# A two-block network on one core, its engines' orders taken from the scheduler's other timing model

## The chip, the cores and the metric

One core of a Trainium2 chip runs the kernel. It has a matrix engine (PE, with weight loads shown apart as PEld), a vector engine (DVE), a scalar engine (ACT), a general engine (POOL) and a sync engine (SP) that only issues transfers. The metric is the device time of one execution in microseconds (us), the median of several runs.

## The reference

Input `x` is 256 tokens of width 1024, all in fp32. The first block is two hybrid layers, the second one mixer layer with routed experts.

```python
def first_block(x, ...):
    for l in range(2):                       # hybrid_layer
        z = rms_norm(x, norm_g) @ w_in       # 2840 columns
        y_a = rg_lru(conv(rg_x)) * silu(rg_gate)
        y_b = nsa(q, k_c, v_c, k_s, v_s, k_w, v_w, ...) * silu(nsa_gate)
        x = x + concat([y_a, y_b]) @ w_out
    return x

def second_block(x, ...):
    p = rms_norm_2(x, norm_mix_w) @ w_in     # 3336 columns
    x = x + concat([rwkv7_mixer(...), fox_mixer(...)]) @ w_out
    h = rms_norm_2(x, norm_ffn_w)
    return x + hierarchical_moe(h, ...)      # top 2 of 64 experts
...
    hid = silu(xblk @ w_gate[e]) * (xblk @ w_up[e])   # 1024 x 512 each
    return hid @ w_down[e]
```

Each of the 64 experts has three matrices of 2 MB, so the experts' weights are some 400 MB.

## The kernel before

The source is one program for the framework's tracer. `model` (L1819) calls the stages in order: `hybrid` twice, `mixer`, then `moe`. Tiles live in one large on-chip array, `arena`, whose places are handed out in Python while the source is traced, in seven blocks `b0` to `b6` of 4096 words, and in PSUM buffers by tag (`mm`, `tp`, `sc`, `ot`, two buffers each).

Dense weights of the first three layers come in blocks through a ring of five of those seven blocks. POOL issues the load of a block (`issue`, L256). Its high part is rounded as it lands. Then `weights_steps` makes the low part: ACT writes the negated high part (L286) and POOL issues a second load of the same words that adds to it (L291). The products of high and low parts are three matmul passes (`mm3_steps`, L304). So each weight block passes through POOL, the DMA engines, ACT, POOL and the DMA engines again before PE can use it all.

Dense products of one branch are used as side work for the other. `step(cols)` runs the generator `self.side` until it has put in matmuls of so many columns; the amounts are constants of the file (`HA` to `HD`, `FA` to `FG`). In `hybrid` the main line is the attention (q, k and v with L501, L502, L507 and L508 as the evictions, L526 and L527 as those of the compressed keys and gates, `rope` L407 to L410, transposes L540, `softmax` L801 to L814, `turned` L822), the side line is `rg_part`. In `mixer` the main line is a triangular solve of 32x32 matmuls (L1057), the side line the remaining projections; L860 to L863 prepare its parameters, which `mixer_params` has SP load (L833).

The experts run in 16 groups of four. Ten slots of 2 MB hold their weights: block 6 and three stretches of the arena as they come free in the mixer, the other six blocks at its end. `fill` has SP issue the next load (L1542, L1557, L1550) as soon as a slot is free in the source; on the chip SP waits in front of each for the last reader of that slot. `experts` gathers rows (L1579), multiplies by gate and up (L1608), and by down (L1639), and adds the result back (L1647, L1649).

What sets the order. Tracing gives one list of instructions with their dependences. When the `tile.TileContext` closes, its scheduler plays this list through a timing model: whenever an engine is free in the model, it takes among the instructions whose inputs the model holds ready the one that comes first in the source. What an engine took one after another becomes its instruction stream, and the waits on other engines are written into it. On the chip an engine goes through its stream in that order, and an instruction that waits holds back those behind it. An instruction marked `keep_in_program_order` is held behind what was traced before it on its engine: the scalings of q and k (L534), the first matmul of the mixer's pinned steps and of each round of the solve, the first gather and one weight block per layer (`PB`).

## Time and profile before

| | us |
|---|---|
| median of 3 runs | 1512.48 (1506.65 to 1514.28) |
| profiled execution | 1520.82 |
| its span, first to last instruction | 1519.1 |
| PE busy | 1217.5 (80%) |
| DVE busy | 423.2 (28%) |
| ACT busy | 316.2 (21%) |
| POOL busy | 148.0 (10%) |
| bytes moved by DMA | 510.27 MB, mean 336 GB/s |

The profile is of one execution. Busy time of PE counts pipelined matmuls as they overlap and isn't PE at its peak. The profile's 40 slices are 38 us each. The first 16 of them are the three dense layers and the routing, the rest are the experts. In the lines of a timeline, the bracket at the end is the idle time of the engine ahead of that instruction, and what ended it.

### The profile page before, as it was taken

To read this page: it belongs to the slowest core of one execution; us is meant where nothing else is said; L and a number is where in the kernel's file an instruction comes from. 1 tells how busy PE (TensorE), PEld (TensorE's weight loads), DVE (VectorE), ACT (ScalarE), POOL (GpSimd) and SP (SyncE) were. 2 spreads that over 40 slices of the span, in tenths; PEclk is the share of its full clock that TensorE was granted. 3 is DMA by queue.
4 is the path that set the end of the run, shared out by engine and by line. 5 is a ranking of instruction groups with operands and counts; after the bars stand their busy time and mean duration, and the time that the engine had idled before them with its cause. 6 is when DMAs were issued, how large, how long until landed. Compare 5 with 4: busy or idle time off the path is not lost.

```text
span 1519.1 us, 20669 instructions
## 1 busy us (share of the span) xinstructions
PE 1217.5 (80%) x8695; PEld 678.3 (45%) x8695; DVE 423.2 (28%) x1250; ACT 316.2 (21%) x748; POOL 148.0 (10%) x201
## 2 busy tenths in 40 slices
PE   6799889889778998976876876877868768768774
PEld 5777677676656685431331331322313313313311
DVE  6546346533525465210110101101101101101010
ACT  4448346736223412000000000000000000000000
POOL 5221322122302300000000000000000000000000
PEclk9979989988899898987987888978878979878897
DMA  8976999749746668999999999999999999999996
GB/s 322 229 190 153 254 281 246 196 129 253 177 99 149 158 230 331 428 427 428 428 428 428 428 428 427 427 428 428 427 428 427 427 429 428 427 429 428 423 408 229
DMA packets 62005, 510.27 MB, mean 336 GB/s; under 512 B 5948, under 2 KB 6076, under 8 KB 34388
## 3 DMA queue, kind: packets, MB, share of 16 engines
q1 hardware_dynamic: 42180, 418.26, 65.7%
q0 software_dynamic: 19728, 90.65, 24.7%
q8 instruction: 70, 1.15, 0.3%
q14 instruction: 27, 0.22, 0.0%
HBM read 507.83 MB, written 1.05 MB: 335 GB/s over the span
## 4 chain that ended last, share of the span: by engine, by line
PE 39%; DMA 33%; DVE 3%; issue 3%; POOL 1%; ACT 0%; POOLq 0%; ACTq 0%; DVEq 0%
DMA slot<-in_wu 19%; DMA arena<-in_wu 12%; PE sc L1608 10%; PE ot L1639 8%; PE tp L1579 8%; PE mm L304 5%; DMA arena<-in_wd 1%; PE tp L1630 1%; DVE arena L1626 1%; PE ot L1057 1%; DMA w<-in_w_in 1%; PE mm L1647 0%; POOL w L291 0%; PE sc L1057 0%; PE sc L1374 0%
## 5 line engine op out<-in xcount | busy, mean ns | idle before, releaser
L1608 PE MATMUL sc<-slot,arena 128*32 128x512 f32 x1424 | 326.6, 741 | 132.5 <-DMA slot<-in_wu 81.4
L1608 PE MATMUL sc<-arena 128*32 128x512 f32 x624 | 187.2, 737 | 61.2 <-DMA arena<-in_wu 37.7
L1608 PEld LDWEIGHTS sc<-slot,arena 128*32 128x32 f32 x1424 | 70.0, 131 | 307.6 <-issue 122.5
L304 PE MATMUL mm<-hT,w 128*128 128x256 f32 (+1 forms) x936 | 142.3, 309 | 4.7 <-DMA w<-in_w_in 3.2
L304 PEld LDWEIGHTS mm<-hT,w 128*128 128x128 f32 (+1 forms) x936 | 127.8, 207 | 17.9 <-issue 9.2
L1579 PEld LDWEIGHTS tp<-arena 128*128 128x128 f32 x512 | 124.3, 334 | 17.9 <-issue 17.9
L1579 PE MATMUL tp<-arena 128*128 128x128 f32 x512 | 128.5, 406 | 2.4 <-DVE arena L1577 2.4
L1639 PE MATMUL ot<-slot,arena 128*32 128x512 f32 x704 | 124.4, 596 | 2.8 <-DMA slot<-in_wd 2.0
L286 ACT ACTIVATE w<-w 128x512 fp32r<-128x512 f32 (+1 forms) x181 | 99.0, 603 | 92.5 <-DMA w<-in_w_in 58.1
L1608 PEld LDWEIGHTS sc<-arena 128*32 128x32 f32 x624 | 40.7, 131 | 166.3 <-issue 76.3
L304 PE MATMUL mm<-w,hT 128*128 128x512 f32 (+1 forms) x432 | 105.1, 396 | 10.7 <-DVE arena L502 4.4
L304 PEld LDWEIGHTS mm<-w,hT 128*128 128x128 f32 x432 | 78.5, 200 | 27.8 <-issue 8.8
L1626 DVE SCALAR_TENSOR_TENSOR arena<-arena,sc 128x512 f32<-128x512 f32 x16 | 11.0, 688 | 265.8 <-PE sc L1608 265.8
L1625 DVE SCALAR_TENSOR_TENSOR arena<-arena,sc 128x512 f32<-128x512 f32 x16 | 11.0, 688 | 265.3 <-ACT arena L1624 265.3
L1649 DVE TENSOR_TENSOR arena<-arena,mm 128x512 f32<-128x512 f32 x64 | 44.0, 688 | 118.2 <-PE mm L1647 118.2
L304 PE MATMUL mm<-w,y 128*128 128x512 f32 x288 | 75.5, 408 | 0.9 <-DVE arena L747 0.9
L1639 PE MATMUL ot<-arena 128*32 128x512 f32 x320 | 71.9, 608 | 3.6 <-DMA arena<-in_wd 3.6
L291 POOL DMA_DIRECT2D w<-in_w_in x67 | 59.5, 946 | 136.5 <-ACT w L286 125.5
L1632 ACT COPY arena<-tp 128x512 f32<-128x512 f32 x16 | 9.4, 586 | 302.7 <-PE tp L1630 302.7
L1644 ACT COPY arena<-ot 128x512 f32<-128x512 f32 x32 | 18.8, 586 | 250.3 <-PE ot L1639 250.3
L1647 PE MATMUL mm<-arena 128*128 128x512 f32 x128 | 64.6, 628 | 1.6 <-ACT arena L1644 1.4
L1624 ACT ACTIVATE arena<-sc 128x512 f32<-128x512 f32 x16 | 9.6, 597 | 261.0 <-PE sc L1608 261.0
(386 smaller groups left out, 1246.8 us busy)
## 6 DMA issues: line engine op xcount, KB each, us to landing
slot<-in_wg SPq DMA_DIRECT2D x47, 2048.0 KB, 31.1
slot<-in_wu SPq DMA_DIRECT2D x42, 2048.0 KB, 33.5
slot<-in_wd SPq DMA_DIRECT2D x42, 2048.0 KB, 35.3
arena<-in_wu SPq DMA_DIRECT2D x22, 2048.0 KB, 33.4
arena<-in_wd SPq DMA_DIRECT2D x18, 2048.0 KB, 34.9
arena<-in_wg SPq DMA_DIRECT2D x17, 2048.0 KB, 32.0
w<-in_w_in POOLq DMA_DIRECT2D x29, 1024.0 KB, 8.7
w<-in_w_in POOLq DMA_DIRECT2D x58, 512.0 KB, 8.8
```

Of the source, the lines that this page charges most:

```text
L286: a = self.S.activation(lo[:, sl], hi[:, sl].bitcast(F32), AF.Copy, scale=-1.0)
L291: self.G.dma_start(lo[:, sl], src[:, sl], accum_op=OP.add)
L304: ins = self.T.matmul(out, lhsT=lhs[k][a], rhs=rhs[k][b], start=(first and i == 0 and k == 0), stop=(last and i == 2 and k == n - 1))
L1057: ins = T.matmul(o[qd(q, d), h * 32:(h + 1) * 32], lhsT=lhs[qd(q, d), h], rhs=rhs[qd(q, d), h], start=True, stop=True)
L1579: ins = T.matmul(self.rows[k // 4][:, k % 4 * 128:(k % 4 + 1) * 128], lhsT=hv[:, tt, k], rhs=D[:, tt], start=(tt == 0 and k % 4 == 0), sto ...
L1608: T.matmul(dst[32 * j:32 * j + 32], lhsT=XT[:, k, 32 * j:32 * j + 32], rhs=w(j), start=(k == 0), stop=(k == 7))
L1626: V.scalar_tensor_tensor(hid, hid, 0.5, pu, OP.mult, OP.mult)
L1630: T.transpose(ps[:, k * 128:(k + 1) * 128], hw[:, k], self.ident)
L1639: T.matmul(py[h][32 * j:32 * j + 32], lhsT=HT[:, k, 32 * j:32 * j + 32], rhs=w(j), start=(k == 0), stop=(k == 3))
L1644: S.copy(Y[:, cs], py[h])
L1647: T.matmul(pc, lhsT=DT[:, tt * 128:(tt + 1) * 128], rhs=Y[:, cs], start=True, stop=True)
L1649: V.tensor_tensor(xs, xs, pc, OP.add)
```

## The change

The one call that opens the scheduler's context gets an argument. With it the scheduler plays the list through the other, finer of its two timing models, when it works out each engine's order. The list itself, its dependences, the pinned instructions, the constants and the places in the arena stay as they were. What can come out otherwise is the order of PE, DVE, ACT, POOL and SP, which of the two PSUM buffers of a tag a tile gets, and the waits that follow from both.

```diff
@@ -1874,6 +1874,6 @@
     out = nc.dram_tensor("out", (1, 256, 1024), F32, kind="ExternalOutput").ap()
-    with tile.TileContext(nc) as tc:
+    with tile.TileContext(nc, schedule_with_timeline_sim=True) as tc:
         model(tc, A, out)
```

## Rows read from the trace of the kernel before

**Rows 1.** The page's 40 slices: busy tenths of the DMA engines

```profile
DMA  8976999749746668999999999999999999999996
```

**Rows 2.** By stretch: busy us of PE, PEld, DVE, ACT, POOL; clock; DMA share; GB/s

```profile
0.00:600.00 600.00, 521.01 (x4927) 412.42 (x4931) 306.01 (x1004) 272.92 (x669) 147.98 (x201) 0.91 0.78 212
600.00:1457.00 857.00, 663.69 (x3592) 258.74 (x3588) 113.05 (x241) 40.92 (x75) 0.00 (x0) 0.85 1.00 426
1457.00:1519.00 62.00, 32.77 (x188) 7.10 (x180) 4.13 (x6) 2.36 (x4) 0.00 (x0) 0.82 0.78 299
```

**Rows 3.** Chain of waits in order of time: start us, us, what

```profile
599.33 13.91 PE sc L1608 x128
...
682.44 30.72 DMA arena<-in_wu
...
740.82 31.11 DMA arena<-in_wu
```

**Rows 4.** Timeline of SP's queue near 590 us: start us, us, instruction

```profile
581.53 0.92 SPq L1557 DMA_DIRECT2D slot<-in_wd  x2
601.24 2.08 SPq L1557 DMA_DIRECT2D arena<-in_wd  x2
```

**Rows 5.** Timeline of PE, [idle before <-releaser]: gaps in the first stage

```profile
41.91 6.46 PE L304 MATMUL mm<-w,hT 128*128 128x280 f32 x48 [0.30 <-ACT arena L512]
...
58.20 1.12 PE L540 MATMUL tp<-arena 128*128 128x128 f32 x4 [5.73 <-DVE arena L410]
...
292.92 4.19 PE L304 MATMUL mm<-w,y 128*128 128x512 f32 x17
302.90 1.51 PE L822 MATMUL tp<-arena 128*128 128x128 f32 x6 [5.79 <-DVE arena L814]
...
332.14 10.27 PE L304 MATMUL mm<-hT,w 128*128 128x256 f32 x72
```

**Rows 6.** Timeline of DVE near 300 us, the same columns

```profile
295.93 0.17 DVE L806 RECIPROCAL arena<-arena 128x4 f32<-128x4 f32 x1
302.17 0.17 DVE L860 TENSOR_SCALAR arena<-arena 128x14 f32<-128x14 f32 x1 [6.08 <-DMA arena<-in_par]
302.26 0.23 DVE L809 TENSOR_TENSOR arena<-arena 128x2 f32<-128x2 f32 x2
```

**Rows 7.** DMA issues: count, KB each, median us from issue to landing

```profile
arena<-in_par SPq DMA_DIRECT2D x1, 597.0 KB, 9.7
...
arena<-in_par SPq DMA_DIRECT2D x1, 332.0 KB, 2.9
...
w<-in_w_in POOLq DMA_DIRECT2D x29, 1024.0 KB, 8.7
```

**Rows 8.** Stretches of 10 us, columns as in rows 2

```profile
50.00:60.00 10.00, 3.36 (x20) 3.16 (x21) 2.32 (x7) 5.31 (x12) 4.66 (x6) 0.81 0.75 215
60.00:70.00 10.00, 9.51 (x66) 8.82 (x66) 7.70 (x22) 6.50 (x15) 1.72 (x3) 0.85 1.06 304
...
250.00:260.00 10.00, 10.00 (x75) 7.30 (x74) 7.09 (x43) 7.11 (x22) 1.24 (x2) 1.00 1.06 288
...
300.00:310.00 10.00, 7.10 (x26) 5.27 (x27) 2.14 (x11) 0.96 (x2) 0.00 (x0) 0.66 0.68 140
...
320.00:330.00 10.00, 6.90 (x34) 5.18 (x32) 5.45 (x12) 3.14 (x8) 1.93 (x5) 1.00 0.26 83
```

**Rows 9.** Timeline of ACT near 52 us, columns as in rows 5

```profile
53.40 2.19 ACT L286 ACTIVATE w<-w 128x512 fp32r<-128x512 f32 x4 [7.62 <-DMA w<-in_w_in]
...
55.75 0.19 ACT L527 ACTIVATE arena<-mm 128x24 f32<-128x24 f32 x1
```

**Rows 10.** Who waited for whom before 620 us: us in total, times, longest

```profile
POOL w L291 <- ACT w L286: 172.1, 40, 24.3
...
ACT w L286 <- DMA w<-in_w_in: 58.1, 18, 10.9
...
PE mm L304 <- DMA w<-in_w_in: 7.5, 5, 2.4
```

## The prediction

> **What bounds the kernel now.** I read first the page's 40 slices: the DMA row stands at 9 from slice 17 on, while its first 16 slices are ragged [rows 1]. The busy time by stretch cuts the span in three [rows 2]. From 600 to 1457 us the DMA engines are full (share 1.00, 426 GB/s) with the expert weights. Before 600 us (two hybrid layers, the mixer, routing) they are at 0.78 and PE is busy 521.01 us. The last 62 us are the end of the weight stream and the final additions. The chain of waits agrees: behind 620 us each group of four experts begins with a wait of some 31 us for `wu`, and these waits stand about 58 us apart (682.44 and 740.82 [rows 3], and so on to the end). So no order of instructions can shorten the middle, as long as slots are given back in time. What an order can move is when the stream goes over into this state. SP's rows show that: at 582 us it has issued the loads of all ten slots, the eleventh load goes out at 601.24, when the first group's matmuls give slots back [rows 4]. Those matmuls start when routing ends, at about 599 us [rows 3]. A first stage that is shorter by D moves the whole expert stage by about D, since the slots come free from the same work. Hence I look for D in the 600 us.
>
> There PE stands idle for 600 - 521 = 79 us [rows 2], the start-up included. That is the most a better order could win by closing gaps. The gaps that I went through by PE's timeline, each with its releaser [rows 5], are of three kinds. (a) Data chains with nothing else ready, such as the normalization between two layers. (b) PE waiting for the weights themselves, 7.5 us in five waits [rows 10]. (c) PE waiting for an engine whose order put an instruction with a late DMA ahead of the one that PE needed. Only (c) is a fault of the order.
>
> **The change, part by part.** No instruction, tile or transfer is added or removed in the source; the arena's addresses are fixed there too. Only the scheduler's idea of when things finish changes, and with it the order of each queue: PE, DVE, ACT, POOL and SP. The trace doesn't show the new orders, so I price what a truer idea of time would mend, and bound the rest.
>
> Mend 1, near 300 us. DVE's rows [rows 6]: the reciprocal of the last softmax (L806) is at 295.93, then DVE waits 6.08 us for L860, which reads the mixer's parameters. Only then come L809 and the scalings of L814, and PE's transposes L822 wait 5.79 us for them [rows 5]. L860 isn't needed there. Its load of 597 KB took 9.7 us to land [rows 7], while a load of 332 KB had landed in 2.9 us at another time. The order before therefore took the load as landed far too soon. PE started 302.90 - 302.26 = 0.64 us after L809. With L860 behind, L809 starts at about 296.1 and PE could go on at 296.7. It is free at 292.92 + 4.19 = 297.11 [rows 5], so nothing of this chain is late any more and the whole 5.8 us is gained. L860 to L863 themselves have time: they feed the mixer's first evictions, and PE begins the mixer's matmuls at 332.14 [rows 5]. The granted clock is 0.66 in 300 to 310 us [rows 8], that is 6.8 us at the lower of its two levels (1.2 GHz). PE's work there would take at most 3.4 us less at 2.4 GHz. Part of the 6.8 us is idle time, so I take 1.
>
> Mend 2, near 52 us. ACT waits 7.62 us for a weight block in front of L286 and runs L526 and L527 behind it, the latter at 55.75 [rows 9]. The matmuls that feed these two ended at 41.91 + 6.46 = 48.37 us [rows 5]. DVE's rope hangs on them through pinned instructions (L530, L534), and its end L410 frees PE's transposes L540 after 5.73 us of idle time [rows 5]. In another order they start as PE runs out: gain up to 5.7 us, and up to 3.4 us of clock (0.81 and 0.85 in 50 to 70 us, again 6.8 us at the lower level). Moving L526 and L527 ahead costs the copy nothing, since it waits for its block until 53.40 anyway, and POOL's reload of that block behind it (L291) goes out no later. But behind it lies a stretch in which the DMA engines are full (1.06 from 60 us on [rows 8]), so the weights could be late next and take it all back. Between 0 and 9.1 I take 3.
>
> The rest. ACT waited 58.1 us in 18 waits for blocks of `w_in` in front of L286, 3.2 us each [rows 10]. Nearly all of it has cover: PE was working on the tiles it had. The DMA waits of kind (b) are worth between 0 and 7.5 us, and I take 0, since nothing shows other work that was ready. New faults: the hand-set amounts of side work and the pinned instructions stay as they were and will meet other orders. Their cost isn't shown; from below 0 (the order also mends what I haven't priced) to +6 each, the size of the two faults above. I take none.
>
> Sum: 5.8 + 1 + 3 = 9.8 us less. The profiled execution took 1520.82 us, a span of 1519.1 and 1.7 around it, and would come to 1511. It is 8.3 us above the median of the three runs, 1512.48, and I hold the difference to be the same for both kernels: 1503 us.
>
> What the Trainium skill says of this: PE's gaps are my measure of the reserve, and PE's busy share is 521 of 600. The Trainium skill ("Perfetto Trace Analysis", Identifying the Most-Contended Engine) calls matmul busy time a bad measure of headroom and takes the share of weight loads instead. That row is 412.42 of 600 [rows 2]; by it the reserve would be 188 us and not 79, and a good order could gain several times my sum. No row shows which order would reach it.
>
> **The rivals.** Rival 1, no change that can be measured: a gap closed in the first stage is lost before 600 us. For it: the DMA engines are at 1.0 or above in 60 to 100 and again through most of 150 to 260 us [rows 8]. Against it: from 300 to 330 us they are at 0.26 to 0.68 [rows 8], so mend 1 isn't behind them. It also holds where the finer model leaves L860 and L286 where they are, so that the orders differ only in places that don't matter. Price: 0 to 6 us less, 1510 us. The Trainium skill ("Perfetto Trace Analysis", Identifying Performance Opportunities) says that kernels gain by the most-contended engine. That is DMA over the whole span here, and by that rule the time would stay at 1512; the trace agrees for 600 us onward.
>
> Rival 2, slower: the weight copies L286 are put further ahead. 181 of them stand in ACT's queue beside the evictions that free PE's two `mm` buffers. It decides once the model takes a reloaded block as landed sooner than the median 8.7 us that the chip needs [rows 7]: then a copy stands in front of an eviction as at 52 us. One such hold costs 3.2 us of ACT, the mean of the 18, and with both buffers full PE shows it whole. If six more of the 18 are no longer covered, that is 6 x 3.2 = 19 us more, 1532 us. For it: POOL already waits 172.1 us for these copies [rows 10], and the amounts of side work were set to the order before. Against it: both faults above come from landings taken as too early, the thing a finer model should be better at.
>
> **How the numbers follow.** Chances: the forecast (mends 1 and 2, wholly or in part) 0.42, rival 1 0.33, rival 2 0.25. The low end is all that I counted plus all bounds: 5.8 + 5.7 of gaps, 3.4 + 3.4 of clock, 7.5 of DMA waits, 25.8 us, so 1487. The high end takes in most of rival 2: five to six holds of 3.2 us, 1530. Both signs are in it; the forecast's own range is 1487 to 1505. About 0.5%, 7.5 us, is what a measurement of this kernel can tell from no change, so faster 0.42, same 0.33, slower 0.25.
>
> **What would show it.** Right: DVE's L860 stands behind L814 and the PE gap near 300 us is gone; ACT's L527 runs straight after its matmuls; SP's eleventh expert load, at 601.24 before, goes out some 10 us sooner; and the waits for `wu` still stand about 58 us apart. Wrong: that load goes out later, with PE waiting for DVE or ACT behind an L286; or it goes out sooner but the DMA share behind it falls under 1.00, which would mean slots come back late. A different time per expert group would overturn the first step.

## The result, and the profile after

| | kernel before | changed kernel |
|---|---|---|
| median of 4 runs each | 1513.34 us (1506.65 to 1514.28) | 1551.78 us (1543.36 to 1558.1) |
| ratio, 95% interval | 1 | 1.0275 (1.0223 to 1.0326) |
| profiled execution, its span | 1520.82, 1519.1 us | 1546.4, 1544.7 us |
| bytes moved by DMA | 510.27 MB | 510.27 MB |
| first expert product (L1608) in the profile | 599.33 us | 627.21 us |

The forecast was 1503 us. The changed kernel is 38 us slower. Executions of one kernel differ: over 29 later runs on one chip the kernel before took 1498.85 to 1520.02 us. Its profiled execution was a slow one (1520.82 us, mean granted clock 0.873) and that of the changed kernel one of its shorter ones (1546.4 us, 0.884), so the profiles lie closer together than the medians. So sizes are taken from medians here, and from profiles what waits for what.

The experiments ran on three chips. The kernel before had medians of 1501.0 us beside the first four runs (ACT alone, PE alone, the two with pins), 1510.93 beside the next four (copies, the other way round, three holds) and 1509.96 beside the last four (stages, mends). Each ratio below is to the kernel before on the same chip.

The same cut into three as in [rows 2], 28 us later (busy us of PE, PEld, DVE, ACT, POOL; granted clock; DMA share; GB/s):

```profile
0.00:628.00 628.00, 538.39 (x4927) 427.01 (x4931) 308.06 (x1005) 271.25 (x669) 149.03 (x201) 0.89 0.75 202
628.00:1485.00 857.00, 682.05 (x3586) 264.29 (x3582) 111.91 (x238) 40.55 (x74) 0.00 (x0) 0.88 1.00 426
1485.00:1544.00 59.00, 30.86 (x194) 7.58 (x184) 5.50 (x8) 2.73 (x5) 0.00 (x0) 0.86 0.82 313
```

The middle is what it was: 857 us, DMA share 1.00, 426 GB/s. The same number of matmuls (x4927) that took 600 us takes 628 us now. The chain of waits of the changed kernel (start us, us, what) and SP's queue say it in the places that the prediction named:

```profile
627.21 13.91 PE sc L1608 x128
...
710.41 30.65 DMA arena<-in_wu
...
770.81 29.35 DMA arena<-in_wu
```

```profile
608.06 0.92 SPq L1557 DMA_DIRECT2D slot<-in_wd  x2
629.12 2.08 SPq L1557 DMA_DIRECT2D arena<-in_wd  x2
```

The waits for `wu` still stand 58 to 61 us apart, and SP's eleventh load, at 601.24 us in [rows 4], goes out at 629.12. All 28 us of the profiles come from the first stage.

There both faults that I had priced are mended. Near 55 us ACT runs L527 straight behind its matmuls, and PE's L540 has no gap. Near 310 us DVE's L860 stands behind the scalings L814 and waits where nobody needs DVE (timelines of ACT, PE and DVE):

```profile
52.29 0.20 ACT L527 ACTIVATE arena<-mm 128x24 f32<-128x24 f32 x1
```

```profile
52.54 3.38 PE L304 MATMUL mm<-hT,w 128*128 128x256 f32 x24 [0.30 <-ACT arena L527]
55.76 0.60 PE L540 MATMUL tp<-arena 128*128 128x128 f32 x4
```

```profile
315.85 1.01 DVE L814 TENSOR_SCALAR arena<-arena 128x128 f32<-128x128 f32 x4
321.27 0.17 DVE L860 TENSOR_SCALAR arena<-arena 128x14 f32<-128x14 f32 x1 [4.41 <-DMA arena<-in_par]
```

But ACT's queue has new faults of the kind of [rows 9]. Three times a block of weight copies L286 waits for its load, and evictions behind it become ready before the copies are done. PE stands for those:

```profile
211.47 2.19 ACT L286 ACTIVATE w<-w 128x512 fp32r<-128x512 f32 x4 [2.95 <-DMA w<-in_w_in]
214.43 2.19 ACT L286 ACTIVATE w<-w 128x512 fp32r<-128x512 f32 x4 [0.76 <-ACT w L286]
...
216.77 0.19 ACT L527 ACTIVATE arena<-mm 128x24 f32<-128x24 f32 x1
...
232.97 2.19 ACT L286 ACTIVATE w<-w 128x512 fp32r<-128x512 f32 x4 [6.84 <-DMA w<-in_w_in]
235.06 0.35 ACT L735 COPY arena<-mm 128x256 f32<-128x256 f32 x1
...
369.68 2.19 ACT L286 ACTIVATE w<-w 128x512 fp32r<-128x512 f32 x4 [7.33 <-DMA w<-in_w_in]
371.77 0.45 ACT L897 ACTIVATE arena<-mm,arena 128x256 f32<-128x256 f32 x1
```

```profile
217.01 7.31 PE L304 MATMUL mm<-hT,w 128*128 128x256 f32 x46 [3.15 <-ACT arena L527]
...
235.93 5.46 PE L304 MATMUL mm<-hT,w 128*128 128x256 f32 x24 [4.30 <-ACT arena L737]
...
372.27 2.07 PE L900 MATMUL mm<-arena 128*128 128x512 f32 x2 [7.48 <-ACT arena L897]
```

In the kernel before the last of the eight L897 started at 348.2 us, before the copies of that block. Around the longest stop, from 364.79 to 372.27 us, the granted clock is at its lower level, 1.2 GHz (columns as in [rows 2]):

```profile
358.00:360.00 2.00, 1.85 (x8) 0.88 (x6) 0.00 (x0) 1.26 (x4) 0.00 (x0) 1.00 1.09 215
360.00:362.00 2.00, 1.85 (x6) 1.20 (x6) 0.00 (x0) 1.19 (x4) 0.00 (x0) 0.68 1.04 205
362.00:364.00 2.00, 2.00 (x4) 0.57 (x3) 1.59 (x3) 0.35 (x1) 0.00 (x0) 0.50 1.09 219
...
376.00:378.00 2.00, 2.00 (x12) 2.00 (x11) 0.00 (x0) 2.00 (x6) 1.72 (x2) 0.56 1.05 209
378.00:380.00 2.00, 2.00 (x19) 2.00 (x18) 0.50 (x3) 1.79 (x5) 0.00 (x0) 1.00 1.06 186
```

By the 0.68 of 360 to 362 us it fell at about 360.7, some 4 us ahead of the stop, so the stop didn't cause the fall, and I can't tell how long the stretch would have been without it.

Summed up, ACT waits longer in front of L286 than the 58.1 us for `w_in` of [rows 10] and the 15.8 for `w_out` (us in total, times, longest):

```profile
ACT w L286 <- DMA w<-in_w_in: 79.4, 17, 10.1
...
ACT w L286 <- DMA w<-in_w_out: 21.9, 9, 7.9
```

PE's own order had changed as well: the last of the main line's matmuls L586, L981 and L990 stand behind more of the side line's L304 than before. The last L586 starts at 252.5 us where it started at 230.0. Which of the two orders costs the 38 us is what the experiments had to tell.

### The profile page after: what moved, and what is told of

It is laid out like the page before. It is cut to its first block, busy times and chain, and to the rows that moved or that the text cites. A ratio compares the mean times of both kernels' runs of the same rounds, so it can differ in the third digit from the quotient of the medians.

```text
span 1544.7 us, 20685 instructions
## 1 busy us (share of the span) xinstructions
PE 1251.3 (81%) x8695; PEld 698.9 (45%) x8695; DVE 425.5 (28%) x1250; ACT 314.5 (20%) x748; POOL 149.0 (10%) x201
## 2 busy tenths in 40 slices
DMA packets 62005, 510.27 MB, mean 330 GB/s; under 512 B 5948, under 2 KB 6076, under 8 KB 34388
## 4 chain that ended last, share of the span: by engine, by line
PE 47%; DMA 37%; issue 7%; POOL 3%; DVE 2%; ACT 2%; POOLq 0%; ACTq 0%; DVEq 0%
DMA slot<-in_wu 17%; DMA arena<-in_wu 12%; PE mm L304 11%; PE sc L1608 10%; PE ot L1639 9%; PE tp L1579 8%; DMA w<-in_w_in 4%; DMA w<-in_w_out 2%; POOL w L291 2%; DMA slot<-in_wg 2%; PE ot L701 1%; PE sc L687 1%; PE tp L822 1%; DMA arena<-in_wd 1%; PE ot L1057 1%
## 5 line engine op out<-in xcount | busy, mean ns | idle before, releaser
L1608 PE MATMUL sc<-slot,arena 128*32 128x512 f32 x1424 | 330.4, 730 | 122.9 <-DMA slot<-in_wu 81.6
L1608 PE MATMUL sc<-arena 128*32 128x512 f32 x624 | 189.4, 726 | 55.1 <-DMA arena<-in_wu 35.4
L1608 PEld LDWEIGHTS sc<-slot,arena 128*32 128x32 f32 x1424 | 72.1, 129 | 290.9 <-issue 120.4
L304 PE MATMUL mm<-hT,w 128*128 128x256 f32 (+1 forms) x936 | 149.2, 317 | 17.6 <-DVE arena L871 5.0
L304 PEld LDWEIGHTS mm<-hT,w 128*128 128x128 f32 (+1 forms) x936 | 133.3, 215 | 34.0 <-issue 10.6
L1639 PE MATMUL ot<-slot,arena 128*32 128x512 f32 x704 | 139.1, 596 | 0.7 <-ACT arena L1632 0.7
L286 ACT ACTIVATE w<-w 128x512 fp32r<-128x512 f32 (+1 forms) x181 | 95.4, 602 | 111.2 <-DMA w<-in_w_in 79.4
L304 PE MATMUL mm<-w,hT 128*128 128x512 f32 (+1 forms) x432 | 103.6, 394 | 15.3 <-DMA w<-in_w_in 9.7
L1608 PEld LDWEIGHTS sc<-arena 128*32 128x32 f32 x624 | 41.1, 129 | 158.3 <-issue 79.4
L304 PEld LDWEIGHTS mm<-w,hT 128*128 128x128 f32 x432 | 78.8, 201 | 31.9 <-issue 6.6
L291 POOL DMA_DIRECT2D w<-in_w_in x67 | 59.2, 917 | 138.8 <-ACT w L286 124.9
L304 PE MATMUL mm<-w,y 128*128 128x512 f32 x288 | 71.2, 398 | 0.3 <-ACT y L234 0.2
L1639 PEld LDWEIGHTS ot<-slot,arena 128*32 128x32 f32 x704 | 34.9, 109 | 68.7 <-issue 61.9
```

Of the source, the lines that this page charges most:

```text
L286: a = self.S.activation(lo[:, sl], hi[:, sl].bitcast(F32), AF.Copy, scale=-1.0)
L291: self.G.dma_start(lo[:, sl], src[:, sl], accum_op=OP.add)
L304: ins = self.T.matmul(out, lhsT=lhs[k][a], rhs=rhs[k][b], start=(first and i == 0 and k == 0), stop=(last and i == 2 and k == n - 1))
L1608: T.matmul(dst[32 * j:32 * j + 32], lhsT=XT[:, k, 32 * j:32 * j + 32], rhs=w(j), start=(k == 0), stop=(k == 7))
L1639: T.matmul(py[h][32 * j:32 * j + 32], lhsT=HT[:, k, 32 * j:32 * j + 32], rhs=w(j), start=(k == 0), stop=(k == 3))
```

## The experiments

Theory A: the loss is in ACT's order, and there in weight copies that stand ahead of evictions (rival 2 of the prediction). Theory B: it is in PE's order, the main line behind the side line. Theory C, a finer question to A: it sits in a few large holds, or in many small ones.

The tool for most runs is a replay. The kernel traces its program twice. The first time the plain model orders it, and each engine's order is noted. The second time chosen engines are held to that order by edges that ask for a place in the queue and for no wait; all else is ordered by the model of that run. Its core:

```diff
+    order = order_of(build(arrays, False))
+    nc = build(arrays, True, order, ("Activation",), None)
...
+    for e in engines:
+        last = None
+        for n in order[e]:
+            if n in at and (stages is None or stage(n) in stages):
+                if last:
+                    tc.add_manual_dep(byname[n], last, info, reason="order of the kernel before")
+                last = n
```

**ACT alone, PE alone.** The first as in the diff, the second with `("PE",)`.

> The finer model orders the program as in the changed kernel, but ACT's instructions are held in the order of the kernel before; PE, DVE, POOL and SP are ordered by the finer model around that. Theory A (the loss is ACT's: weight copies L286 stand further ahead, wait for their loads and hold evictions behind them; in the changed kernel the three such holds at 213.86, 231.63 and 364.79 us leave PE idle 3.15, 4.30 and 7.48 us, and a stretch at the lower clock follows): the time comes back to 1520 us or less, the first expert products (L1608) to 605 us or less from 627.21. Theory B (the loss is PE's own order: matmuls of the side line L304 stand ahead of the main line's L586 to L643, L981 and L990): little comes back, 1540 us or more, L1608 at 620 us or later.

> As the run before, but PE alone is held in the order of the kernel before; ACT, DVE, POOL and SP are ordered by the finer model around that. Theory B: 1520 us or less, L1608 at 605 us or sooner. Theory A: 1535 us or more, with PE idle more often behind an eviction that stands behind a waiting L286.

ACT in the old order: 1522.96 us, ratio to the kernel before on the same chip 1.0112 (1.0055 to 1.017), L1608 at 603.8 us. PE in the old order: 1550.38 us, 1.0308 (1.0261 to 1.0355), L1608 at 620.8. So ACT's order gives back some six tenths of the loss, where the intervals leave room for a quarter to eight tenths. PE's gives nothing in the sum, though it brings the main line's matmuls back to their places. With PE's order held, the hold at the head of the mixer is as long as ever: three of the eight L897 stand behind copies, and PE waits in the midst of its L895.

```profile
361.83 1.22 PE L895 MATMUL mm<-arena 64*128 64x256 f32 x2 [7.68 <-ACT arena L897]
```

The run with ACT's order missed its bound of 1520, by 3 us as it stands and by more against this chip's 1501.0: about 1% stays with the orders of the other engines.

**All copies at their place in the source.** If copies stand too far ahead, pin each behind the ACT instruction traced before it, in both kernels:

```diff
-        n = 4 if m > 1024 else 1
+        n, pin = 4 if m > 1024 else 1, True
```

> The changed kernel with every weight copy L286 pinned behind the ACT instruction that was traced before it, so that a copy can't be moved ahead of that eviction. Theory A: 1525 us or less, ACT's idle time at L286 for loads falls from 79.4 us. Theory B: within 6 us of the changed kernel's 1552 us; the copies come later, and L304 waits for its weights in their stead.

> The same pins on the kernel before, so that the price of the pins by themselves is seen. Theory A: pins on a kernel in which few copies stand ahead of evictions change little, 1505 to 1520 us. If pinned copies make weights late, both kernels lose by them: 1525 us or more here, and the run before can't speak against theory A.

The pins make both kernels slower: 1575.14 us, 1.0467 (1.0419 to 1.0515), on the finer model, and 1534.01 us, 1.02 (1.0152 to 1.0248), on the plain one. So the first can't speak against A, as its counterpart was there to tell. It shows the other side of the same choice. On the finer model ACT's waits fall, and PE waits for weights instead, 47.2 us after 12.9 in the changed kernel and 7.5 in [rows 10]:

```profile
PE mm L304 <- DMA w<-in_w_in: 47.2, 15, 7.3
ACT w L286 <- DMA w<-in_w_in: 33.6, 5, 9.4
```

A copy too early holds evictions. A copy too late makes POOL's reload (L291) late, and PE with it: POOL waits 226.3 us for copies where it waited 173.7 in the changed kernel. With the copies pinned alike, the two models' kernels are still 41 us apart. So where copies are late, other orders of the finer model cost as well, and which of them wasn't tried.

**Copies not further ahead; and the reverse.** In the first of two runs each copy is held behind those ACT instructions that stand ahead of it in the kernel before, and may come later; nothing else is held. In the second all but the copies keep the old order.

```diff
+    for k, n in enumerate(names):
+        if n in COPIES:
+            for b in [b for b in names[:k] if b not in COPIES][-60:]:
+                tc.add_manual_dep(byname[n], b, info, reason="order of the kernel before")
```

> The finer model orders the program, and each weight copy L286 is held behind those of ACT's other instructions that stand ahead of it in the kernel before; it may come later than there, and ACT's other instructions are free. Theory A: most of what the whole of ACT's order gave back comes back, 1530 us or less. If it is the order of the evictions among themselves that costs, 1545 us or more. If copies are made late by it, PE waits for weights (L304 behind L286 or behind a load) where it waited for evictions.

> The counterpart: all of ACT's instructions but the copies L286 are held in the order of the kernel before among themselves, the copies are placed by the finer model. Theory A: little comes back, 1545 us or more, with ACT's idle time at L286 for loads still near 79 us and evictions behind it. If it is the order of the evictions that costs: 1530 us or less.

Copies not ahead: 1524.1 us, 1.0077 (1.0042 to 1.0112). All others in order, copies free: 1557.17 us, 1.0321 (1.0254 to 1.0387). That is A, by both. In these two runs ACT's waits for `w_in` in front of L286 go with it, here first the run with copies held, then the one with the others held:

```profile
ACT w L286 <- DMA w<-in_w_in: 41.6, 10, 9.4
```

```profile
ACT w L286 <- DMA w<-in_w_in: 84.1, 21, 10.6
```

Over all runs their sum is no measure of the time: it is 62.8 us with PE as before (1.0308), and 73.0 in a run below that loses 0.4%.

**The other way round.** The plain model orders the program, ACT alone has the order that the finer model gave it.

> The other way round: the plain model orders the program as in the kernel before, but ACT is held in the order that the finer model gave it. If ACT's order carries the loss whatever the other engines do: 1530 us or more, L1608 at 615 us or later from 599.33. If ACT's order is bad only together with the order of PE that came with it: 1520 us or less.

1553.99 us, 1.0301 (1.0236 to 1.0367), L1608 at 628.5: ACT's order alone, with the other engines ordered around it by the plain model, brings the whole loss into the kernel before.

**Three holds taken out.** The changed kernel's own order on all engines, replayed, but the three blocks of copies shown above stand behind the evictions that they held. The numbers are the first copy, the count, and how many other instructions the block is put behind:

```diff
+    order = mended(order_of(build(arrays, True)), ((76, 8, 4), (84, 8, 5), (129, 4, 5)), False)
...
+    for k, n, by in later:
+        part = copies[k:k + n]
+        after = [i for i in act[act.index(part[0]):] if i not in set(COPIES)][by - 1]
+        for i in part:
+            act.remove(i)
+        at = act.index(after) + 1
+        act[at:at] = part
```

> The changed kernel's own order on all engines, with one edit: three blocks of weight copies L286, those that wait at 211.47, 232.97 and 369.68 us, stand behind the evictions that they held (L526 and L527; L735, L737 and L546; the last L897, L901, L914 and L915). Theory A (ACT's loss is these few holds): PE's idle 3.15, 4.30 and 7.48 us go, 14.9 together, and some of the time at the lower clock behind them; L1608 at 613 us or sooner from 627.21, 1537 us or less. Theory C (ACT's order costs in many small places, or one hold only uncovers the next): 5 us or less come back, L1608 at 622 us or later.

1548.01 us, 1.0255 (1.0186 to 1.0324), L1608 at 627.0: next to nothing of 14.9 us, as C had it. The interval by itself would leave room for much of them, but the trace shows where they went: PE stands idle 92.0 us until L1608, after 89.6 in the changed kernel. At the first place the 3.15 us for L527 become 2.16 and 1.72 us for the weights. At the mixer's head the eight L897 run early now, PE finishes L900 without a stop, and then waits 6.30 us for the second L901, which stands behind the same block and the next one:

```profile
369.86 2.19 ACT L286 ACTIVATE w<-w 128x512 fp32r<-128x512 f32 x4 [2.35 <-DMA w<-in_w_in]
372.36 2.19 ACT L286 ACTIVATE w<-w 128x512 fp32r<-128x512 f32 x4 [0.32 <-DMA w<-in_w_in]
...
374.56 0.56 ACT L901 COPY arena<-mm 128x512 f32<-128x512 f32 x1
```

```profile
375.18 7.72 PE L304 MATMUL mm<-hT,w 128*128 128x256 f32 x48 [6.30 <-ACT arena L901]
```

Near 235 us the 4.30 us for L737 become 3.44 for DVE's L747, which follows an L746 behind three such blocks. In the three places together 14.9 us become 13.6. Where most copies stand too far ahead, one that is moved uncovers the next.

**Stage by stage.** All engines in the order of the kernel before, in the two hybrid layers alone, then in the mixer alone.

> The finer model orders the program, but in the two hybrid layers every engine's instructions stand in the order of the kernel before. Which stage loses: the changed kernel is 13.8 us late at the end of the norm that follows the hybrid layers (L348, 331.9 to 345.7) and 27.9 at L1608. If a stage's loss is its own, 10 to 17 us of the 38 to 40 come back, 1535 to 1542 us, and L348 ends at 334 us or sooner. If only the whole order helps: 1545 us or more.

> The counterpart: in the mixer every engine's instructions stand in the order of the kernel before, the hybrid layers are the finer model's. If a stage's loss is its own: 1530 to 1542 us, L348 ends at 343 to 347 us and L1608 starts 262 to 272 us behind it, as in the kernel before (267.4), not 281.5 as in the changed one. If only the whole order helps: 1545 us or more.

Hybrid layers as before: 1512.58 us, 1.0036 (1.0001 to 1.0071). Mixer as before: 1529.49 us, 1.0137 (1.0083 to 1.019), L1608 260.9 us behind the end of L348. The first run gave back more than the 10 to 17 us expected, and the second lies just under both its ranges. The finer model's hybrid layers cost 21 us by the second run, which has mend 1 in it. Its mixer costs 5 by the first; L860 to L863 are traced in the mixer, so this run has mend 1 in it too, and without its some 6 us (an estimate from the gap of 5.79) the mixer costs about 11. Together that is 32 of the 38 to 41 us. The intervals are 5 to 8 us either way, so a cost of the two together is neither shown nor excluded. The largest stop in the mixer is the same hold again, 7.71 us of PE:

```profile
327.11 1.22 PE L895 MATMUL mm<-arena 64*128 64x256 f32 x2 [7.71 <-ACT arena L897]
```

**The mends alone.** The order of the kernel before on all engines, with mends 1 and 2 and nothing else; then with two more holds taken out.

```diff
+    order = mended(order_of(build(arrays, False)), ((12, 4, 2),), True)
...
+    if params:
+        for i in PARAMS:
+            dve.remove(i)
+        at = max(dve.index(i) for i in SCALED[:64]) + 1
+        dve[at:at] = PARAMS
```

`PARAMS` are L860 to L863, `SCALED` are the L814. The second run has `((12, 4, 2), (100, 4, 6), (137, 3, 2))`, where the third moves three copies; the fourth of their block stood behind L921 already.

> The order of the kernel before on all engines with the two mends of the prediction alone: L860 to L863 stand behind the last L814 (mend 1), and the four weight copies L286 that waited at 53.40 us stand behind the L526 and L527 that they held (mend 2). By the prediction's sum: PE's idle 5.79 us near 297 and 5.73 us near 52 go, L1608 starts at 588 to 592 us from 599.33, and the time is 7 to 11 us under the kernel before. If a mended hold is only followed by the next late thing: PE's two gaps are gone, but L1608 starts within 3 us of 599 and the time is within 4 us of the kernel before.

> As the run before, and two more blocks of weight copies put behind the evictions that they hold: the one at 258.17 us behind the L803 and the two L828 after it (PE idle 1.93 us at 261.06), and the one at 367.54 us behind L870 and L921 (PE idle 3.36 us at 366.66). If each hold costs its gap: 5 us less than the run before, 12 to 16 us under the kernel before, the shortest time of all. If the next late thing takes its place: the same as the run before.

Two mends: 1501.64 us, 0.9947 (0.992 to 0.9974), 8.3 us under the kernel before by the medians. It beats both kernels. The two mends weren't run apart. PE has no gap at mend 1, L860 waits behind all that PE needs. Mend 2 closes its gap at L540 too, but part of it comes back 4 us later, behind the two blocks that now follow each other (DVE, ACT, PE):

```profile
288.48 1.01 DVE L814 TENSOR_SCALAR arena<-arena 128x128 f32<-128x128 f32 x4
293.83 0.18 DVE L860 TENSOR_SCALAR arena<-arena 128x14 f32<-128x14 f32 x1 [4.34 <-DMA arena<-in_par]
```

```profile
47.01 0.20 ACT L527 ACTIVATE arena<-mm 128x24 f32<-128x24 f32 x1
50.04 2.20 ACT L286 ACTIVATE w<-w 128x512 fp32r<-128x512 f32 x4 [2.83 <-DMA w<-in_w_in]
```

```profile
289.10 0.89 PE L822 MATMUL tp<-arena 128*128 128x128 f32 x6
...
56.25 0.58 PE L304 MATMUL mm<-hT,w 128*128 128x256 f32 x1 [2.91 <-ACT arena L737]
58.13 1.09 PE L540 MATMUL tp<-arena 128*128 128x128 f32 x4 [1.30 <-DVE arena L410]
```

Four mends: 1502.14 us, 0.9943 (0.9912 to 0.9975), the same, though a gain of a few us would not show in these intervals. Its two extra gaps (1.93 and 3.36 us of PE) are gone from the trace, but PE's idle time until L1608 is 68.3 us after 67.5 with two mends. At the first place the wait has moved from L822 to the L759 behind it and lasts from 251.96 us, as the moved block now holds L762:

```profile
254.02 1.08 PE L759 MATMUL mm<-arena 64*64 64x256 f32 x8 [2.06 <-ACT arena L762]
```

## Where the copies stand, and the time

The built orders can be compared copy by copy: how many of ACT's other instructions stand ahead of a copy, against the kernel before. For the 181 copies:

| kernel | copies further ahead | copies later | ratio |
|---|---|---|---|
| ACT as before (finer model) | 0 | 0 | 1.0112 |
| copies not ahead (finer model) | 0 | 75 | 1.0077 |
| hybrid layers as before | 40 | 0 | 1.0036 |
| mixer as before | 85 | 20 | 1.0137 |
| PE as before | 105 | 12 | 1.0308 |
| changed kernel | 121 | 20 | 1.0275 |
| others in order | 119 | 12 | 1.0321 |
| pins, plain model | 1 | 159 | 1.02 |
| pins, finer model | 5 | 160 | 1.0467 |

In the changed kernel 121 of 181 copies stand further ahead, and only 20 later; the mean over all 181 is 7 places further ahead. On the finer model the two runs with none further ahead cost about 1% or less, the ones with 40 and 85 cost 0.4 and 1.4%, those with over 100 cost 3%. So do two runs that aren't in the table: ACT's changed order on the plain model has the changed kernel's 121 (1.0301), and with three holds out there are 107 by the order in its trace (1.0255). The pins mark the far end, with most copies late, and there the counts don't tell 1.02 from 1.0467.

PE's time until the first L1608 shows how the time is lost (one execution each, columns as in [rows 2], the kernel before and the changed one):

```profile
0.00:599.33 599.33, 520.34 (x4923) 412.21 (x4927) 305.34 (x1003) 272.55 (x668) 147.98 (x201) 0.91 0.78 212
```

```profile
0.00:627.21 627.21, 537.61 (x4923) 426.79 (x4927) 307.27 (x1003) 270.88 (x668) 149.03 (x201) 0.89 0.75 202
```

PE stands idle 79.0 us in the one and 89.6 in the other, of which some 10 and some 26 us end with ACT. The idle time is 102.9 us with PE as before and 105.1 with the others in order, but 75.3 with copies not ahead. That fits A. It isn't all: PE is also busy 17.3 us longer with the same matmuls. The trace has 102 and 108 us of the busy time at the lower clock, which by my estimate (half of the difference) explains some 3 of the 17. The rest goes with PE's own order. Busy time less half of its part at the lower clock is 469 to 474 us in the kernel before, with PE as before, with the hybrid layers as before and with the mends. It is 479 to 484 us in the changed kernel, with ACT as before, copies not ahead, the others in order and three holds out. These 10 us or so are close to the 1% that stays when ACT's order or the copies alone are put right; with PE as before they come back, and PE's longer waits take them. Why the same matmuls take longer in the finer model's order isn't shown.

The run the other way round loses its time differently: PE is idle 82.2 us and busy 546.3, with 134 us of that at the lower clock. That ACT's order costs it 3% is measured; that it does so by PE's waits isn't shown there.

## Why the prediction was wrong

**The middle, and D.** Right. The first stage came out 27.9 us longer in the profile and the last `wd` wait of the stream ends 27.8 us later, with the DMA engines full between. With two mends it held for a shorter first stage as well: the time fell.

**Mend 1 and mend 2.** Right in kind, and the finer model made both, as forecast. Their sum was 9.8 us; alone they give 8.3 by the medians (4 to 12 by the interval). Mend 2 is the smaller for what it uncovers, 2.91 + 1.30 us where 5.73 were: 1.5 us of gap, half of the 3 that I took.

**"The rest": new faults, "I take none".** This is the step that failed. I bounded a new fault by +6 each and then gave no number of them, though the change could re-order all 181 copies (it moved 141) and I had priced only two faults in the order that was there. As what the mends leave unexplained, if they give here what they give alone, the term measured 38.4 + 8.3, some 47 us. A second thing was put at nothing without a reason: my measure of the reserve was PE's gaps, so PE's work counted as the same in any order, and in the profiles it is some 14 us more at equal clock. The DMA waits of PE, taken as 0 with a bound of 7.5 on the side of a gain, went the other way too: PE's waits for `w_in` rose from 7.5 to 12.9 us.

**Rival 2** is what happened for the larger part: copies ahead of evictions, PE waiting for ACT behind an L286, the eleventh load later. Its price, six holds of 3.2 us, was too small, and its form didn't fit. The run with three holds taken out shows that holds don't add up like that; the order of all copies counts. And its chance was too low, I think, for one reason. Against it I put that "a finer model should be better at" landings. No row said so: a guess on the model's quality stood against a mechanism with a row.

**Rival 1** named a gap that is closed and lost again. This did happen to the three holds, to mend 2 in part, and to the third and fourth mends, but not to mend 1.

**The weight-load rule.** The Trainium skill ("Perfetto Trace Analysis", Identifying the Most-Contended Engine) would have PE's reserve read from weight loads, and from the share of peak FLOPs, which I left out. By weight loads alone I estimated 188 us in 600. The reserve that orders reached here is 8 us in one direction; no run got near 188, and none was made to look for it.

**Left open.** What in the finer model puts copies ahead isn't seen in a trace; that it takes loads as landed sooner is a guess. How the 38 us divide is known from single executions only: in the two profiles 10.6 of the 27.9 us are PE standing still, some 3 the lower clock and some 14 PE's longer work. That a stop is followed by a stretch at the lower clock, as the expectations have it, is not shown, since the one looked at began before its stop.

## What to carry to other kernels

An in-order queue that serves two masters, here evictions for PE and copies for the weight pipeline, is priced by its order as a whole and not by the holds that show in the trace: in the order in which most copies stood too far ahead, taking out the largest holds uncovered the next. In the good order two single moves paid and two more showed no gain. When a scheduler's model changes, expect every such queue to be dealt anew, and give "new faults" a number before counting the mends; a first guess is as many as the old order has. PE's busy time isn't fixed under such a change either. A good order is worth keeping as data: hold it by edges, move single instructions that a trace shows in front of a late load, and measure.

## What was not expected of the hardware

The granted clock of a stretch is not set by the order alone. In 80 to 100 us three kernels have the same order on PE, DVE and POOL, and on ACT but for mend 2 in the last: the kernel before, the one with hybrid layers as before, and the one with two mends.

```profile
80.00:100.00 20.00, 18.34 (x86) 14.54 (x84) 8.04 (x34) 8.58 (x24) 4.59 (x6) 0.67 1.06 265
```

```profile
80.00:100.00 20.00, 19.59 (x129) 14.66 (x129) 14.77 (x73) 13.88 (x44) 4.39 (x6) 1.00 0.91 218
```

```profile
80.00:100.00 20.00, 18.44 (x69) 13.97 (x68) 9.66 (x42) 7.93 (x25) 4.01 (x5) 0.57 0.89 203
```

The clock was 0.67, 1.00 and 0.57, and 86, 129 and 69 matmuls were done. The stretches don't hold quite the same work; counted in PE's common order, the matmuls from the 401st to the 500th took 26.8, 16.7 and 26.6 us. The last L501 of layer 1 ran at 184.5, 169.8 and 182.1 us. So two profiles of one order can be 15 us apart by 180 us.

The 24.5 us by which L1608 came sooner with two mends in the profile (574.8 against 599.33, sooner than the 588 to 592 expected) are thus not the mends' 8.3 alone. PE's idle time gives 11.5 of them (79.0 to 67.5). The rest is busy time, of which 73 us lie at the lower clock after 102: half of that difference, some 14 us, accounts for it (an estimate).
